# Casting x on VectorE with a loop staggered over four batches, loads and stores in order on one queue: a masked softmax of 16 matrix products

## The chip, the cores and the metric

The kernel runs on 1 core of a Trainium2 chip. The metric is the device time in microseconds (us), median of several runs; the profile covers one execution of them and its span is some 1.8 us shorter than the time measured for that execution (before: 92.4 of 94.16). Engines: PE = TensorE, DVE = VectorE, ACT = ScalarE, POOL = GpSimd, SP = the sync engine, which here only issues transfers. A profile page cuts the span into 40 equal slices: a digit of an engine's row is its busy time in tenths, PEclk is the clock that TensorE was granted in tenths of its full speed, DMA the busy share of the transfer engines, GB/s what they moved.

## The reference

```python
batch, m, k, n = 16, 512, 512, 512          # x float32, weight [k, n], scale 0.125
y = scale * np.matmul(x, weight)
y = np.where(mask == 1, y, -1e9)            # mask: strictly below the diagonal
y_exp = np.exp(y - np.max(y, axis=-1, keepdims=True))
return y_exp / np.sum(y_exp, axis=-1, keepdims=True)
```

A batch brings 1 MB of x in and takes 1 MB of result out. The exponentials are small enough here that the kernels leave the maximum out.

## The kernel before

For each batch: load x, cast to bf16 on the way by a GpSimd transfer; transpose its 16 blocks on TensorE (`prepare`); copy the transposed halves from PSUM to SBUF, one on VectorE, one on ScalarE; multiply block row by block row, only up to the diagonal, with one more matmul that adds a mask of -512 on the diagonal block; exponentiate on ScalarE, with row sums; scale by the reciprocal of the sums on VectorE; store.

```python
X_BUFS = 16
    def load(b):
        xb = x_pool.tile([P, MT, K], BF16, name="xb")
        nc.gpsimd.dma_start(xb, x_r[b])
    ...
    def prepare(b):                                  # 16 transposes, two copies
        for h in range(2):
            pt = psum_t.tile([P, 2, M], BF16, name="pt")
            ...
            if h == 0: nc.vector.tensor_copy(xt[:, 0:2], pt)
            else:      nc.scalar.copy(xt[:, 2:4], pt)
    ...
    def normalise(b):
        nc.vector.reciprocal(rinv, st_sum.pop(b))
        for mt in range(MT):
            NC = (mt + 1) * P
            nc.vector.tensor_scalar_mul(ot[:, mt, :NC], ot[:, mt, :NC], rinv[:, mt : mt + 1])
    ...
    for b in range(B):
        if b + 1 < B: prepare(b + 1)
        multiply(b); normalise(b); store(b)
```

The program is not run in the order of its source. Each engine's instructions are put into an order when the program is built, and each engine then runs its list from top to bottom.

The softmax here doesn't subtract the row's maximum and nothing guards it: scores larger than these inputs give would overflow.

Of the kernel before, what the change touches and what calls it, by code (L numbers as in the profile page):

```python
# [1 line left out]

# [5 lines left out]

FP32 = mybir.dt.float32
BF16 = mybir.dt.bfloat16  # L10
AF = mybir.ActivationFunctionType
ALU = mybir.AluOpType

MASK_NEG = -512.0
P = 128
X_BUFS = 16
OUT_BUFS = 6


@with_exitstack  # L20
def kernel(
    ctx: ExitStack,
    tc: tile.TileContext,
    x: bass.AP,
    weight: bass.AP,
    scale: float,
    mask: bass.AP,
    out: bass.AP,
):






    nc = tc.nc

    B, M, K = x.shape
    K2, N = weight.shape
    assert K == K2 and N == 512 and K == 512 and M == 512  # L40
    MT = M // P
    KT = K // P

    const = ctx.enter_context(tc.tile_pool(name="const", bufs=1))
    x_pool = ctx.enter_context(tc.tile_pool(name="xf", bufs=X_BUFS))
    xt_pool = ctx.enter_context(tc.tile_pool(name="xt", bufs=2))
    sum_pool = ctx.enter_context(tc.tile_pool(name="sums", bufs=4))
    psum_t = ctx.enter_context(tc.tile_pool(name="psum_t", bufs=4, space=bass.MemoryType.PSUM))
    psum_y = ctx.enter_context(tc.tile_pool(name="psum_y", bufs=4, space=bass.MemoryType.PSUM))

    x_r = x.rearrange("b (mt p) k -> b p mt k", p=P)
    out_r = out.rearrange("b (mt p) n -> b p mt n", p=P)

    ident_bf = const.tile([P, P], BF16, name="ident_bf")
    w_f32 = const.tile([P, KT, N], FP32, name="w_f32")
    w_bf = const.tile([P, KT, N], BF16, name="w_bf")
    diag_f32 = const.tile([P, MT, P], FP32, name="diag_f32")
    diag_bf = const.tile([P, MT, P], BF16, name="diag_bf")
    ots = [const.tile([P, MT, N], FP32, name=f"ot{i}") for i in range(OUT_BUFS)]

    st_x, st_xt, st_py, st_sum = {}, {}, {}, {}

    def load(b):
        xb = x_pool.tile([P, MT, K], BF16, name="xb")
        nc.gpsimd.dma_start(xb, x_r[b])  # L65
        st_x[b] = xb

    def prepare(b):

        xb = st_x.pop(b)  # L70
        xt = xt_pool.tile([P, KT, M], BF16, name="xt")
        for h in range(2):
            pt = psum_t.tile([P, 2, M], BF16, name="pt")
            for kk in range(2):
                kt = 2 * h + kk
                for mt in range(MT):
                    nc.tensor.transpose(  # L77
                        pt[:, kk, mt * P : (mt + 1) * P],
                        xb[:, mt, kt * P : (kt + 1) * P],
                        ident_bf,  # L80
                    )
            if h == 0:
                nc.vector.tensor_copy(xt[:, 0:2], pt)  # L83
            else:
                nc.scalar.copy(xt[:, 2:4], pt)  # L85
        st_xt[b] = xt

    def multiply(b):
        xt = st_xt.pop(b)
        ot = ots[b % OUT_BUFS]  # L90
        rsum = sum_pool.tile([P, MT], FP32, name="rsum")
        for mt in range(MT):
            NC = (mt + 1) * P
            py = psum_y.tile([P, N], FP32, name="py")
            for kt in range(KT):
                nc.tensor.matmul(  # L96
                    py[:, :NC],
                    lhsT=xt[:, kt, mt * P : NC],
                    rhs=w_bf[:, kt, :NC],
                    start=(kt == 0),  # L100
                    stop=(kt == KT - 1),
                )
            nc.tensor.matmul(  # L103
                py[:, mt * P : NC],
                lhsT=ident_bf,
                rhs=diag_bf[:, mt],
                start=False,
                stop=True,
                skip_group_check=True,
            )  # L110
            nc.scalar.activation(  # L111
                out=ot[:, mt, :NC],
                in_=py[:, :NC],
                func=AF.Exp,
                bias=0.0,
                scale=float(scale),
                accum_out=rsum[:, mt : mt + 1],
            )
        st_sum[b] = rsum

    def normalise(b):
        ot = ots[b % OUT_BUFS]
        rinv = sum_pool.tile([P, MT], FP32, name="rinv")
# [4 lines that stand above are left out]
        nc.gpsimd.memset(ot[0:1, 0, :P], 1.0 / N)  # L128

    def store(b):  # L130
        nc.sync.dma_start(out_r[b], ots[b % OUT_BUFS])  # L131

    make_identity(nc, ident_bf)


    load(0)
    nc.sync.dma_start(w_f32, weight.rearrange("(kt p) n -> p kt n", p=P))
    for mt in range(MT):
        nc.sync.dma_start(diag_f32[:, mt], mask[mt * P : (mt + 1) * P, mt * P : (mt + 1) * P])
    for b in range(1, X_BUFS):  # L140
        load(b)

    for ot in ots:
        for mt in range(MT - 1):
            nc.gpsimd.memset(ot[:, mt, (mt + 1) * P :], 0.0)  # L145
        nc.gpsimd.memset(ot[0:1, 0, P:], 1.0 / N)  # L146

    prepare(0)
    for kt in range(KT):
        if kt % 2 == 0:  # L150
            nc.vector.tensor_copy(w_bf[:, kt], w_f32[:, kt])  # L151
        else:
            nc.scalar.copy(w_bf[:, kt], w_f32[:, kt])  # L153
    nc.vector.tensor_scalar(  # L154
        out=diag_bf,
        in0=diag_f32,
        scalar1=-MASK_NEG,
        scalar2=MASK_NEG,
        op0=ALU.mult,
        op1=ALU.add,  # L160
    )

    for b in range(B):
        if b + 1 < B:
            prepare(b + 1)
        multiply(b)
        normalise(b)
        store(b)
        if b + X_BUFS < B:
            load(b + X_BUFS)  # L170


# [1 line left out]
_INS = ['x', 'weight', 'scale', 'mask']  # L174
_OUTS = [((16, 512, 512), 'float32')]

_NUMBERS = {'scale': 0.125}


# [26 lines left out]
```

## Time and profile before

| | before |
|---|---|
| time, median | 94.33 us |
| span | 92.4 us |
| busy PE / ACT / DVE | 57.5 / 47.0 / 37.2 us |
| bytes through HBM | 34.87 MB |
| a batch's compute, where nothing holds it (57 to 80 us) | 3.29 us |
| a batch's transfers at 408 GB/s | 5.14 us |

The row DMA of the page (tenths of busy time in 40 slices) is full all through, and the compute engines are not: the transfers are the bound. The lines are in the prediction below.

### The profile page before, as it was taken

The page shows a single profiled execution, that of the slowest core. Times are in us where ns is not written, and L with a number is a line of the kernel's source. Part 1 is how long each engine was busy: PE and PEld are TensorE (multiplying, and loading weights), DVE is VectorE, ACT ScalarE, POOL GpSimd, SP SyncE. Part 2 cuts the span into 40 slices and gives each one's busy share as a digit, 9 for nine tenths or more (in the row PEclk, how much of TensorE's full clock was granted, in tenths as well). Part 3 has the DMA queues.
Part 4 walks back from the last instruction along what each step waited for, and adds up shares of the span by engine and source line. Part 5 has one row for each costly group of instructions (what it writes and reads, how often), then busy time and mean ns, then how long its engine had stood idle before and what let it go on. Part 6 is the DMA issues. An engine that isn't in the chain of part 4 may idle for free.

```text
span 92.4 us, 1586 instructions
## 1 busy us (share of the span) xinstructions
PE 57.5 (62%) x568; PEld 43.1 (47%) x576; DVE 37.2 (40%) x99; ACT 47.0 (51%) x147; POOL 25.3 (27%) x62
## 2 busy tenths in 40 slices
PE   0000599999999999900019774699999999600000
PEld 0000568867876876900016352576786786200000
DVE  0030212458546799300004217276845853650000
ACT  5040044998789873400034091899878878700000
POOL 5993333222333999800001001011101110110000
PEclk9999999999999999996555699999999999995555
DMA  1899999999999999999999999999999999999990
GB/s 27 335 220 191 208 206 206 206 206 207 206 206 207 208 208 206 206 206 283 290 286 291 285 337 403 397 407 403 408 406 407 401 407 407 409 408 410 408 353 33
DMA packets 18007, 26.57 MB, mean 288 GB/s; under 512 B 592, under 2 KB 9296, under 8 KB 18000
## 3 DMA queue, kind: packets, MB, share of 16 engines
q0 software_dynamic: 8448, 8.39, 54.7%
q1 hardware_dynamic: 9552, 18.09, 52.5%
q8 instruction: 4, 0.07, 0.3%
q14 instruction: 3, 0.02, 0.1%
HBM read 18.09 MB, written 16.78 MB: 377 GB/s over the span
## 4 chain that ended last, share of the span: by engine, by line
DMA 44%; PE 23%; POOL 17%; DVE 1%; issue 1%; ACT 1%; DVEq 0%; SPq 0%; ACTq 0%; POOLq 0%
DMA xb<-in_x_dram 24%; DMA out_dram<-ot 20%; PE py L96 17%; POOL xb L65 7%; POOL ot L145 7%; PE pt L77 5%; POOL ot L146 2%; PE py L103 2%; DVE ot L127 1%; ACT ot L111 1%; POOL ot L128 1%; POOL ident_bf masks.py:199 0%; DVEq L201 0%; SPq L131 0%; POOL ident_bf masks.py:197 0%
## 5 line engine op out<-in xcount | busy, mean ns | idle before, releaser
L96 PE MATMUL py<-w_bf,xt 128*128 128x128 bf16 (+3 forms) x248 | 42.6, 310 | 12.2 <-ACT ot L111 11.6
L111 ACT ACTIVATE ot<-py 128x128 f32<-128x128 f32 (+1 forms) x64 | 27.5, 443 | 18.2 <-DMA out_dram<-ot 14.9
L96 PEld LDWEIGHTS <-xt 128*128 128x128 bf16 x256 | 22.2, 102 | 21.5 <-issue 13.4
L77 PE MATMUL pt<-ident_bf,xb 128*128 128x128 bf16 x256 | 18.1, 230 | 10.2 <-DMA xb<-in_x_dram 10.2
L127 DVE TENSOR_SCALAR ot<-ot,rinv 128x128 f32<-128x128 f32 (+1 forms) x64 | 23.2, 445 | 1.6 <-DVE rinv L124 0.5
L85 ACT COPY xt<-pt 128x1024 bf16<-128x1024 bf16 x16 | 16.2, 1016 | 10.8 <-PE pt L77 8.5
L77 PEld LDWEIGHTS <-xb 128*128 128x128 bf16 x256 | 16.3, 104 | 11.6 <-DMA xb<-in_x_dram 10.2
L83 DVE COPY xt<-pt 128x1024 bf16<-128x1024 bf16 x16 | 11.0, 689 | 15.9 <-PE pt L77 14.2
L65 POOL DMA_DIRECT2D xb<-in_x_dram x16 | 12.2, 770 | 16.4 <-DMA xb<-in_x_dram 16.1
L128 POOL MEMSET ot<- 1x128 f32 x16 | 4.3, 287 | 39.4 <-DVE ot L127 39.4
L103 PE MATMUL py<-diag_bf,ident_bf 128*128 128x128 bf16 x64 | 14.4, 225 | 0.0
L111 ACT ACTIVATION_READ_ACCUMULATOR ot<-py 128x1 f32 x64 | 13.4, 210 | 0.0
L124 DVE RECIPROCAL rinv<-rsum 128x4 f32<-128x4 f32 x16 | 2.7, 172 | 18.1 <-ACT ot L111 18.1
L103 PEld LDWEIGHTS <-ident_bf 128*128 128x128 bf16 x64 | 6.5, 102 | 3.4 <-issue 0.5
L145 POOL MEMSET ot<- 128x384 f32 (+2 forms) x18 | 6.3, 383 | 0.0
L151 DVE CAST w_bf<-w_f 128x512 bf16<-128x512 f32 x2 | 0.9, 481 | 5.9 <-DMA w_f<-in_weight_dram 5.9
L153 ACT CAST w_bf<-w_f 128x512 bf16<-128x512 f32 x2 | 1.1, 616 | 3.9 <-DMA w_f<-in_weight_dram 3.9
L146 POOL MEMSET ot<- 1x384 f32 x6 | 2.4, 408 | 0.0
L154 DVE TENSOR_SCALAR diag_bf<-diag_f 128x512 bf16<-128x512 f32 x1 | 0.4, 427 | 3.6 <-DMA diag_f<-in_mask_dram 3.6
L153 ACT ACT_TABLE_LOAD x1 | 1.3, 1283 | 0.7 <-PEq L187 0.7
masks.py:199 POOL TENSOR_SCALAR_AFFINE_SELECT ident_bf<-ident_bf 128x128 bf16<-128x128 bf16 x1 | 0.3, 307 | 0.1
masks.py:197 POOL MEMSET ident_bf<- 128x128 bf16 x1 | 0.2, 206 | 0.3 <-POOLq L187 0.3
(4 smaller groups left out, 0.4 us busy)
## 6 DMA issues: line engine op xcount, KB each, us to landing
out_dram<-ot SPq DMA_DIRECT2D x16, 1024.0 KB, 11.6
xb<-in_x_dram POOLq DMA_DIRECT2D x16, 512.0 KB, 21.0
w_f<-in_weight_dram SPq DMA_DIRECT2D x1, 1024.0 KB, 5.1
diag_f<-in_mask_dram SPq DMA_DIRECT2D x4, 64.0 KB, 6.5
```

The source lines that it names most:

```text
L65: nc.gpsimd.dma_start(xb, x_r[b])
L77: nc.tensor.transpose(pt[:, kk, mt * P : (mt + 1) * P], xb[:, mt, kt * P : (kt + 1) * P], ident_bf,)
L83: nc.vector.tensor_copy(xt[:, 0:2], pt)
L85: nc.scalar.copy(xt[:, 2:4], pt)
L96: nc.tensor.matmul(py[:, :NC], lhsT=xt[:, kt, mt * P : NC], rhs=w_bf[:, kt, :NC], start=(kt == 0), stop=(kt == KT - 1),)
L103: nc.tensor.matmul(py[:, mt * P : NC], lhsT=ident_bf, rhs=diag_bf[:, mt], start=False, stop=True, skip_group_check=True,)
L111: nc.scalar.activation(out=ot[:, mt, :NC], in_=py[:, :NC], func=AF.Exp, bias=0.0, scale=float(scale), accum_out=rsum[:, mt : mt + 1],)
L124: nc.vector.reciprocal(rinv, st_sum.pop(b))
L127: nc.vector.tensor_scalar_mul(ot[:, mt, :NC], ot[:, mt, :NC], rinv[:, mt : mt + 1])
L128: nc.gpsimd.memset(ot[0:1, 0, :P], 1.0 / N)
L145: nc.gpsimd.memset(ot[:, mt, (mt + 1) * P :], 0.0)
L146: nc.gpsimd.memset(ot[0:1, 0, P:], 1.0 / N)
```

## The change

The cast leaves the transfer and becomes a VectorE instruction; x is loaded as fp32 on the same queue that stores the results; the loop is staggered so that at step i the cast is for batch i+2, the transposes for i+1, the multiplication for i and the normalisation for i-1. The buffers for x go from 16 (bf16) to 5 (fp32).

```diff
-X_BUFS = 16
+X_BUFS = 5
     def load(b):
-        xb = x_pool.tile([P, MT, K], BF16, name="xb")
-        nc.gpsimd.dma_start(xb, x_r[b])
+        xf = x_pool.tile([P, MT, K], FP32, name="xf")
+        nc.sync.dma_start(xf, x_r[b])
+    def cast(b):
+        xb = xb_pool.tile([P, MT, K], BF16, name="xb")      # 3 buffers
+        nc.vector.tensor_copy(xb, st_x.pop(b))
 ...
-    for b in range(B):
-        if b + 1 < B:
-            prepare(b + 1)
-        multiply(b)
-        normalise(b)
-        store(b)
+    for i in range(B + 1):
+        if i + 2 < B:
+            cast(i + 2)
+        if i + 1 < B:
+            transpose(i + 1)
+        if i < B:
+            multiply(i)
+        if i >= 1:
+            normalise(i - 1)
+            store(i - 1)
+            if i - 1 + X_BUFS < B:
+                load(i - 1 + X_BUFS)
```

(Cut: set-up of the pool for the cast tiles, `cast(0)`, `transpose(0)` and `cast(1)` ahead of the loop, and the identity matrix made after the loads are issued.)

More of the change, by code (lines that the diff above doesn't have):

```diff
@@ L45 @@
     x_pool = ctx.enter_context(tc.tile_pool(name="xf", bufs=X_BUFS))
+    xb_pool = ctx.enter_context(tc.tile_pool(name="xb", bufs=3))
     xt_pool = ctx.enter_context(tc.tile_pool(name="xt", bufs=2))
@@ L59, with transpose @@
     ots = [const.tile([P, MT, N], FP32, name=f"ot{i}") for i in range(OUT_BUFS)]
-    st_x, st_xt, st_py, st_sum = {}, {}, {}, {}
+    st_x, st_xb, st_xt, st_sum = {}, {}, {}, {}
     def load(b):
-        xb = x_pool.tile([P, MT, K], BF16, name="xb")
-        nc.gpsimd.dma_start(xb, x_r[b])
-        st_x[b] = xb
-    def prepare(b):
-        xb = st_x.pop(b)
+        xf = x_pool.tile([P, MT, K], FP32, name="xf")
+        nc.sync.dma_start(xf, x_r[b])
+        st_x[b] = xf
+    def cast(b):
+        xb = xb_pool.tile([P, MT, K], BF16, name="xb")
+        nc.vector.tensor_copy(xb, st_x.pop(b))
+        st_xb[b] = xb
+    def transpose(b):
+        xb = st_xb.pop(b)
         xt = xt_pool.tile([P, KT, M], BF16, name="xt")
@@ L131, in store @@
         nc.sync.dma_start(out_r[b], ots[b % OUT_BUFS])
-    make_identity(nc, ident_bf)
     load(0)
@@ L141 @@
         load(b)
+    make_identity(nc, ident_bf)
     for ot in ots:
@@ L146 @@
         nc.gpsimd.memset(ot[0:1, 0, P:], 1.0 / N)
-    prepare(0)
+    cast(0)
+    transpose(0)
     for kt in range(KT):
@@ L161 @@
     )
-    for b in range(B):
-        if b + 1 < B:
-            prepare(b + 1)
-        multiply(b)
-        normalise(b)
-        store(b)
-        if b + X_BUFS < B:
-            load(b + X_BUFS)
+    cast(1)
+    for i in range(B + 1):
[10 more added lines that the diff above has]
+                load(i - 1 + X_BUFS)
 _INS = ['x', 'weight', 'scale', 'mask']
```

## The prediction

> **What bounds the kernel now.** I read the page first (slices, queues), then busy time by stretch, then the timeline, for the duration of each step.
>
> ```profile
> span 92.4 us, 1586 instructions
> ...
> PE   0000599999999999900019774699999999600000
> ...
> PEclk9999999999999999996555699999999999995555
> DMA  1899999999999999999999999999999999999990
> GB/s 27 335 220 191 208 206 206 206 206 207 206 206 207 208 208 206 206 206 283 290 286 291 285 337 403 397 407 403 408 406 407 401 407 407 409 408 410 408 353 33
> ...
> HBM read 18.09 MB, written 16.78 MB: 377 GB/s over the span
> ```
>
> One slice is 2.31 us. The DMA row is full from the second slice to the last but one; TensorE has two idle stretches that cost nothing. In slices 5 to 18 only loads run: 206 GB/s counted as bf16 landed, so 412 GB/s of fp32 read. From slice 25 only stores run, at some 407. Between, the mixture moves 290 counted. Everything is 18.09 + 16.78 = 34.87 MB, and 34.87 / 0.408 = 85.5 us: the transfers are the bound, with about 7 us of start, first slices and end around them. The compute engines need much less: PE 57.5, ACT 47.0, DVE 37.2 us busy, and in the stretch from 57 to 80 us a batch takes 3.29 us (transposes start at 64.24 and again at 67.53), with TensorE the limit. A batch's transfers need 2.097 MB / 0.408 = 5.14 us. So compute has 1.85 us to spare per batch, if its steps overlap.
>
> The lengths of those steps, from the timeline (start, length, engine, line, operation, count):
>
> ```profile
> 64.19 0.22 PE L103 MATMUL py<-diag_bf,ident_bf 128*128 128x128 bf16 x1
> ...
> 64.24 1.06 PE L77 MATMUL pt<-ident_bf,xb 128*128 128x128 bf16 x16
> ...
> 64.89 0.69 DVE L83 COPY xt<-pt 128x1024 bf16<-128x1024 bf16 x1 [0.86 <-PE pt L77]
> ...
> 67.47 0.22 PE L103 MATMUL py<-diag_bf,ident_bf 128*128 128x128 bf16 x1
> ...
> 67.73 0.60 ACT L111 ACTIVATE ot<-py 128x512 f32<-128x512 f32 x1 [0.23 <-PE py L103]
> ...
> 80.72 0.18 DVE L124 RECIPROCAL rinv<-rsum 128x4 f32<-128x4 f32 x1 [0.83 <-ACT ot L111]
> 80.99 1.29 DVE L127 TENSOR_SCALAR ot<-ot,rinv 128x128 f32<-128x128 f32 x4
> ```
>
> From the first transpose to the copy that empties the first half: 0.65 us (64.24 to 64.89). The batch's matmuls: 65.14 (first line of that group) to 67.47 + 0.22, so 2.55 us. Last exponential to reciprocal: 80.00 to 80.72, so 0.72. Reciprocal to first scaling: 0.27; four scalings: 1.29.
>
> **What the Trainium skill says.** "DMA: Bandwidth & Descriptors", section "SWDGE vs HWDGE vs iDMA": a cast during a DMA can only be issued from GpSimd; plain transfers may go by the sync queue. Section "Issuing engines are not separate DMA queues": all issuers share the same 16 engines. The trace agrees as far as it goes: software-queue loads read 412 GB/s, hardware-queue stores write 408. So I give the new queue no gain in rate. "VectorE: DVE Perf Modes", section "The perf-mode tier table": an fp32 SBUF copy of 2048 elements takes 1227 ns. The trace has no such size; its two casts of 512 took 0.88 us together, 0.44 each, and 1536 more elements at two per cycle of 0.96 GHz (the page's clock) add 0.80: 1.24. I take 1.23, an estimate. "TensorE: Matmul & The Clock Gate", Part 1: an idle array falls to half clock and needs a stretch of work to recover. The trace agrees: after TensorE stopped at 39.35 us the granted clock was 0.50 from 43 us, and it stayed so until 52, over 3 us into the next work.
>
> **The change part by part.**
> - Removed: the bf16 cast in the loads; 16 issues on GpSimd of 0.77 us. Neither bounds anything but the first 9 us, where slices 2 to 4 moved only about 2.1 MB of source data in 6.9 us. Worth about 1.7 us at the start (7 us at 408 GB/s would move 2.8 MB).
> - Moved: x as fp32 on the sync queue, 5 buffers instead of 16. Bytes through HBM are unchanged. After the first five, load n+5 is issued behind store n.
> - Added: 16 casts on VectorE, 16 x 1.23 = 19.7 us: 37.2 + 19.7 = 57 us of 92, no bound by itself.
> - The stagger: the source lets the cast run two batches ahead and the normalisation one behind. But the built program isn't in source order. I listed VectorE's instructions as built (batch numbers counted by me):
>
> ```
> Reciprocal(6)  cast(7)  scale(6) x3  copy xt(7)  scale(6)
> Reciprocal(7)  scale(7)  cast(8)  scale(7) x3  copy xt(8)
> Reciprocal(8)  cast(9)  scale(8) x3  copy xt(9)  scale(8)
> ```
>
> From batch 5 on, the cast of n+1 stands **behind the reciprocal of n**, except cast 11, ahead of reciprocal 10. TensorE's built order is transposes(n), all matmuls(n), transposes(n+1). An engine runs in order, so a closed ring arises: reciprocal(n) -> cast(n+1) -> transposes(n+1) -> copy to xt -> matmuls(n+1) -> last exponential -> reciprocal(n+1). Nothing of one batch overlaps the next in it, and prefetched loads can't shorten it.
>
> Length of the ring, when the cast follows at once: reciprocal to next operation 0.20; cast 1.23; three scalings 0.90 (longer than the 0.65 for the first transposes, so they hide it); copy 0.69; weight load 0.06 (11.99 to 12.05 in the start of the trace); matmuls 2.55; 0.03 to the exponential; 0.72. Sum 6.38 us. The other half of xt, on ScalarE, is ready about 0.94 + 0.2 + 1.02 = 2.2 us after the cast, while the matmuls that need only the first half run, and adds nothing. With one scaling ahead of the cast: 0.27 + 0.25 + 1.23 + 1.0 + 0.69 + 0.06 + 2.55 + 0.75 = 6.80. With the cast already done: 0.27 + 0.90 + 0.69 + 0.06 + 2.55 + 0.75 = 5.22. Reciprocal 5 to 15 is five of 6.80, four of 6.38 and one of 5.22: 64.7 us, against 51.4 that the transfers would need.
>
> The start: the first load is issued at about 0.75 and lands near 5.5 (the weights took 5.1 from issue to landing), the weights behind it near 8.1, their casts and the first copy end near 10, and the first matmuls run at half rate (the trace's first 16 transposes took 1.89 us instead of 1.06), so reciprocal 0 comes near 14.8. The casts are a batch or two ahead there; walking the built lists step by step with the same lengths puts reciprocal 5 near 36. End: 36 + 64.7 = 100.7; scaling 0.27 + 1.29; the last store of 1 MB alone some 4.7 (an estimate from the 5.1 of the weights); span 107. The measured time was 94.33 for a span of 92.4, so 1.9 more: **109 us**, 15% slower.
>
> **The rivals.**
> - *Transfers still bound it.* Five loads are in flight and 5.14 us a batch is generous; if the ring is under 5.1 us, the span is about 2.1 + 34.87 / 0.405 + 0.7 for a bubble ahead of the last stores + 2 = 91, time 92.8. Mixing loads and stores could cost some: between 47.75 and 53.17 the mixture moved 290 counted, about 190 of it store (one store's buffer came free at each of those times), so 390 of source, 4% under the pure rates; then 94 to 95. For it: DMA has always been the bound. Against: it needs 1.2 to 1.7 us off a sum of measured steps.
> - *VectorE's total is the bound*: per batch 1.23 + 0.69 + 0.27 + 1.29 = 3.5 us, below 5.14. No.
> - *The clock falls.* In the ring TensorE works 0.94 + 2.4 of 6.6 us with a pause of about 2.4 us. In the trace the clock fell 3 to 3.7 us after work stopped, so I expect it to hold. If it fell for good, matmuls and transposes add about 3 us per batch: 120 and more.
>
> **Range and chances.** The ring's sum has seven terms good to about 0.3 us together: ten rounds, 3 us; the start is good to 3 us; a lowered clock now and then adds up to 7. So 102 to 116. A prediction within 2% needs the ring to be wrong by 1.2 us a batch: 0.04; faster by 2% needs also a better transfer rate: 0.03.
>
> **What would show it.** Right: DMA row at 7 to 8 tenths in the middle, DVE waiting in total tens of us on ACT (at the reciprocal), TensorE waiting on DVE casts, periods of 6.3 to 6.8 us between reciprocals, cast at 1.2 us, no long wait of the casts for loads. Wrong: a full DMA row and casts that wait for loads (the first rival), or PEclk at 5 for most of the span (the third). The estimate fails most easily if the cast isn't 1.23 us, or if loads land so late that the ring isn't what ends last.

## The result

The changed kernel takes 114.94 us (113.28 to 116.26, 4 runs, the two longest of them counted as slow), before 94.33 (94.16 to 94.41). The ratio is 1.209, 95% interval 1.195 to 1.223. Ratios here are the mean time of one kernel's fast runs over that of the other's fast runs in the same rounds, so not quite the ratio of the medians. The time lies inside the predicted range of 102 to 116, at its upper end, 6 us above the predicted 109.

The page of the changed kernel, the rows that answer to those shown of before (here a slice is 2.83 us):

```profile
span 113.0 us, 1605 instructions
...
PE   0009959999765593846928379483956928379000
...
DVE  0076367796781904629055392608219045380500
...
PEclk9999999999999769996799958999596799958985
DMA  2998999999999999999999999989970900909072
GB/s 26 375 384 292 402 388 387 399 387 359 273 372 411 399 408 407 409 409 410 404 410 409 395 395 405 337 308 252 391 279 6 352 19 20 351 16 355 0 282 89
```

The GB/s row holds to the 25th slice; from the 31st on there are single transfers with nothing between. From the 15th slice on PE and DVE tend to take turns (9 over 0, 9 over 0 again, 2 over 5, 9 over 2): a first sign that they wait for each other. The waits (engine, line, what it waited for: total us, times, longest):

```profile
DVE rinv L131 <- ACT ot L118: 42.1, 14, 4.4
...
PE pt L84 <- DVE xb L73: 30.7, 12, 8.3
...
DVE xb L73 <- DMA xf<-in_x_dram: 8.3, 2, 6.1
```

VectorE waits 42 us at the reciprocal for the exponentials; TensorE waits 31 us for casts; the casts themselves waited for a load only twice, in the start. The data was there. One round of the ring, from the timeline:

```profile
57.76 0.18 DVE L131 RECIPROCAL rinv<-rsum 128x4 f32<-128x4 f32 x1 [4.14 <-ACT ot L118]
57.85 1.20 DVE L73 CAST xb<-xf 128x2048 bf16<-128x2048 f32 x1
...
59.10 1.07 PE L84 MATMUL pt<-ident_bf,xb 128*128 128x128 bf16 x16 [2.10 <-DVE xb L73]
...
59.78 0.67 DVE L90 COPY xt<-pt 128x1024 bf16<-128x1024 bf16 x1
...
60.51 1.16 PE L103 MATMUL py<-w_bf,xt 128*128 128x128 bf16 x9 [0.34 <-DVE xt L90]
...
63.12 0.60 ACT L118 ACTIVATE ot<-py 128x512 f32<-128x512 f32 x1
...
63.84 0.18 DVE L131 RECIPROCAL rinv<-rsum 128x4 f32<-128x4 f32 x1 [2.99 <-ACT ot L118]
```

Read the starts downwards: every line begins when the one above it has delivered what it needs or has freed its engine, and the last line is the first one again, one batch and 6.08 us later. The transfers of a batch would need 5.14.

Not every round is so short. Of the ten from reciprocal 5 (36.34 us) to reciprocal 15 (105.55 us), six take 7.5 to 7.7 us. The stretches of 1 us around one of them show why (columns: stretch, length, busy us and instructions of PE, weight loads, DVE, ACT and POOL, granted clock, DMA share, GB/s):

```profile
50.00:51.00 1.00, 0.00 (x0) 0.00 (x0) 0.81 (x3) 0.07 (x1) 0.28 (x1) 1.00 1.06 410
51.00:52.00 1.00, 0.15 (x2) 0.15 (x3) 1.00 (x3) 0.00 (x0) 0.93 (x1) 0.79 1.05 410
52.00:53.00 1.00, 1.00 (x12) 1.00 (x11) 0.88 (x4) 0.00 (x0) 0.00 (x0) 0.50 1.04 404
...
54.00:55.00 1.00, 0.93 (x6) 0.28 (x5) 0.00 (x0) 0.83 (x1) 0.00 (x0) 0.50 1.04 395
55.00:56.00 1.00, 1.00 (x11) 0.78 (x11) 0.00 (x0) 0.65 (x4) 0.00 (x0) 1.00 1.06 410
```

TensorE paused for about 2.5 us while VectorE scaled and cast, its clock fell to one half, and the transposes and the first matmuls ran at that rate for 3 us. In the five rounds with a scaling ahead of the cast the pause was 2.45 to 2.51 us, and the clock fell each time. But with the cast directly behind the reciprocal it was 2.10 to 2.11 us, and there the clock fell in one round of four, when the transposes already ran:

```profile
77.96 1.07 PE L84 MATMUL pt<-ident_bf,xb 128*128 128x128 bf16 x16 [2.10 <-DVE xb L73]
```

```profile
78.00:79.00 1.00, 1.00 (x16) 0.85 (x16) 1.00 (x4) 0.00 (x0) 0.34 (x1) 0.94 0.84 227
79.00:80.00 1.00, 0.66 (x6) 0.52 (x6) 0.70 (x2) 0.90 (x1) 0.00 (x0) 0.50 1.03 352
```

So the length of the pause doesn't decide alone. The falls come at 37.93, 51.58, 65.24, 78.89, 85.72 and 99.37 us: two or four times 3.41 us lie between one and the next, and each low stretch lasts 3.41 us. This points to a fixed grid of time, on which it matters where a pause lies; no run here moved a pause on purpose. The four runs line up with their mean clock: 0.908 for 113.28 us, 0.894 and 0.895 for 114.81 and 115.06, 0.881 for 116.26.

### The profile page after: what moved, and what is told of

The parts are those of the page before. It is cut to its first block, busy times and chain, and to the rows that moved or that the text cites. A ratio compares the mean times of both kernels' runs of the same rounds, so it can differ in the third digit from the quotient of the medians.

```text
span 113.0 us, 1605 instructions
## 1 busy us (share of the span) xinstructions
PE 68.6 (61%) x576; PEld 46.2 (41%) x576; DVE 53.7 (47%) x115; ACT 49.3 (44%) x147; POOL 18.3 (16%) x46
## 5 line engine op out<-in xcount | busy, mean ns | idle before, releaser
L103 PE MATMUL py<-w_bf,xt 128*128 128x512 bf16 (+3 forms) x256 | 47.2, 330 | 5.5 <-DVE xt L90 5.0
L84 PE MATMUL pt<-ident_bf,xb 128*128 128x128 bf16 x256 | 22.0, 254 | 30.7 <-DVE xb L73 30.7
L84 PEld LDWEIGHTS <-xb 128*128 128x128 bf16 x256 | 18.8, 116 | 35.0 <-DVE xb L73 34.8
L73 DVE CAST xb<-xf 128x2048 bf16<-128x2048 f32 x16 | 20.4, 1273 | 8.3 <-DMA xf<-in_x_dram 8.3
L135 POOL MEMSET ot<- 1x128 f32 x16 | 9.8, 614 | 87.7 <-DVE ot L134 75.0
L134 DVE TENSOR_SCALAR ot<-ot,rinv 128x128 f32<-128x128 f32 (+1 forms) x64 | 21.8, 385 | 0.8
L118 ACT ACTIVATION_READ_ACCUMULATOR ot<-py 128x1 f32 x64 | 12.8, 200 | 0.0
```

Of the source, the lines that this page charges most:

```text
L73: nc.vector.tensor_copy(xb, st_x.pop(b))
L84: nc.tensor.transpose(pt[:, kk, mt * P : (mt + 1) * P], xb[:, mt, kt * P : (kt + 1) * P], ident_bf,)
L103: nc.tensor.matmul(py[:, :NC], lhsT=xt[:, kt, mt * P : NC], rhs=w_bf[:, kt, :NC], start=(kt == 0), stop=(kt == KT - 1),)
L118: nc.scalar.activation(out=ot[:, mt, :NC], in_=py[:, :NC], func=AF.Exp, bias=0.0, scale=float(scale), accum_out=rsum[:, mt : mt + 1],)
L135: nc.gpsimd.memset(ot[0:1, 0, :P], 1.0 / N)
```

## The experiments

**Theory.** VectorE's built order (cast of n+1 behind the reciprocal of n) closes a ring through three engines (VectorE, TensorE, ScalarE), and the ring's length is the period. **Rival A:** five buffers and one queue in order starve the transfers. **Rival B:** VectorE has simply too much to do. All experiments give correct results. "Held" below means that each instruction is pinned behind the previous one of its engine in source order; that fixes the list:

```diff
+    keep = tc.keep_in_program_order
-        nc.vector.tensor_copy(xb, st_x.pop(b))
+        keep(nc.vector.tensor_copy(xb, st_x.pop(b)))
 (the same for every instruction on VectorE, TensorE, ScalarE and for the transfers on SP)
```

| run | order on VectorE | x buffers | median us | ratio to before |
|---|---|---|---|---|
| changed kernel | as built: cast behind the reciprocal | 5 | 114.94 | 1.209 |
| e1_source_order | held, source: cast two batches ahead of the multiplication, three ahead of the reciprocal | 5 | 112.59 | 1.191 |
| e5_source_order_6 | the same | 6 | 99.22 | 1.051 |
| e2_source_order_10 | the same | 10 | 96.19 | 1.019 |
| e8_source_10_cast_twice | the same, each cast twice | 10 | 95.89 | one run |
| e3_ring_10 | held: cast behind the reciprocal | 10 | 163.26 | 1.731 |
| e7_ring_10_warm | the same, extra matmuls in the pause | 10 | 128.09 | one run |
| e4_cast_early_5 | held: cast just ahead of the reciprocal | 5 | 103.77 | 1.100 |
| e6_ten_buffers_only | as built | 10 | 96.14 | 1.021 |
| e9_best_7, e10_best_8 | held, source, start mended | 7, 8 | 95.91, 95.85 | 1.017, 1.017 |

The kernel before took 94.3 to 94.4 us beside all of them.

### e1: the order of the source, five buffers

> The changed kernel with every VectorE, TensorE, ScalarE and sync-queue instruction held in the order of its source (cast two batches ahead of the normalisation, on every batch), still 5 x buffers. Theory (a closed ring through VectorE's built order sets the period): the ring is cut, reciprocals come every 5.1 to 6 us, time 95 to 103 us. Rival A (5 buffers and one queue in order starve the transfers): nothing changes, 113 to 116. Rival B (VectorE has too much work): the work is the same, so 113 to 116.

Measured 112.59 us: outside the theory's range and near the rivals'. The ring is gone, and another limit appears at nearly the same time. One line of its waits, then of its timeline:

```profile
DVE xb L74 <- DMA xf<-in_x_dram: 43.6, 15, 6.3
```

```profile
56.87 1.23 DVE L74 CAST xb<-xf 128x2048 bf16<-128x2048 f32 x1 [2.48 <-DMA xf<-in_x_dram]
...
62.37 1.23 DVE L74 CAST xb<-xf 128x2048 bf16<-128x2048 f32 x1 [2.20 <-DMA xf<-in_x_dram]
```

From 44.85 us on each cast waits over 2 us for its load. The cast of batch n+3 stands ahead of the scaling of n, hence of store n, hence of load n+5, which is behind the store on the queue and needs the buffer. So only two periods lie between the landing of load n+3 and that of load n+5. The nine reciprocals from 46.59 to 94.30 us come every 5.96 us on average. Casting further ahead uses the prefetch up: rival A is right for this order, though not for the built one.

### e5 and e2: six and ten buffers

```diff
-X_BUFS = 5
+X_BUFS = 6      # e5;  10 in e2
```

> As e1_source_order with one x buffer more (6). In e1 a second ring showed: load n+5 is issued behind store n, which stands behind the cast of n+3, so only two periods lie between the landing of load n+3 and of load n+5: 2 x 5.9 us measured. Theory: with 6 buffers there are three periods, 11.7 / 3 = 3.9 us, below the 5.14 us of the transfers, so these bind again: 95 to 97 us, like e2. Rival (5 buffers were not the reason, something in the single queue was): 105 or more.

> As e1_source_order, with 10 x buffers instead of 5. Theory: the transfers are the bound again, DMA row full, 91 to 95 us. If e1 stays above 97 and this one falls to 91 to 95, then behind the ring lay a second limit, the number of x buffers. Rival B (VectorE's total): 110 or more.

With one buffer more 99.22 us, with ten 96.19, 2.2 and 1.2 us above the expected ranges (95 to 97, 91 to 95). With six, reciprocals come every 5.1 us from the sixth on (45.05, 50.13, 55.20), so the steady state is that of the transfers, as expected; what it loses against e2 it loses around the fourth reciprocal (28.01, then 34.35), where slices 10 to 13 of its page move only 263 to 338 GB/s, and at the end, where slices 35 to 39 move 278 to 382. With ten, the page of e2 shows the transfers full to the end:

```profile
DMA  2897999999999999999999999999999999999940
GB/s 27 333 402 214 365 402 388 388 385 388 388 385 386 386 400 411 392 408 408 405 408 402 409 408 409 408 410 408 408 402 407 408 406 411 407 410 406 411 174 7
```

So the staggered loop works as intended only with order and buffers both: 96.19 us, and even then 1.9% above the kernel before.

### e3 and e7: the ring with ten buffers, without and with work in its pause

The source was rewritten so that it names VectorE's built order, the same for all batches, and was held (shortened: guards and keep left out):

```diff
 def normalise(b):
     nc.vector.reciprocal(rinv, st_sum.pop(b))
+    cast(b + 1)
     for mt in range(MT):
+        if mt == MT - 1: transpose(b + 1)
         nc.vector.tensor_scalar_mul(...)
-for i in range(B + 1): ...
+for b in range(B): multiply(b); normalise(b); store(b); load(b + X_BUFS)
-X_BUFS = 5
+X_BUFS = 10
```

> The order in which the changed kernel was built, made regular by hand for all batches (cast of n+1 behind the reciprocal of n, TensorE strictly transposes, matmuls, transposes), held so, with 10 x buffers. Theory: more prefetch can't shorten the ring; periods of 6.1 to 7.7 us for all 15 steps, 115 to 126 us. Rival A (buffers starve the transfers): 92 to 98.

Measured 163.26 us: prefetch doesn't help the ring at all, so rival A is out for the built order; but the theory had expected 115 to 126. Part of the difference is TensorE's list. The built program runs first the matmuls that need only VectorE's half of xt; held in source order, each batch also waits 0.4 to 0.8 us for ScalarE's half. The clock row of its page and two reciprocals:

```profile
PEclk9999955585585559576556858555765955555685
```

```profile
62.74 0.18 DVE L132 RECIPROCAL rinv<-rsum 128x4 f32<-128x4 f32 x1 [5.38 <-ACT ot L119]
72.20 0.18 DVE L132 RECIPROCAL rinv<-rsum 128x4 f32<-128x4 f32 x1 [6.14 <-ACT ot L119]
```

A round takes 8.9 to 9.8 us, most of it at half clock. To see whether the clock is the cause, e7 puts 24 matmuls into the pause; nobody reads their result, and they only add work:

```diff
+    dummy = psum_d.tile([P, P], FP32, name="dummy")        # psum_t: 3 buffers instead of 4
 def multiply(b):
     ...
+    for _ in range(24):
+        nc.tensor.matmul(dummy, lhsT=ident_bf, rhs=ident_bf, start=True, stop=True)
```

> e3_ring_10 with 24 extra matmuls (identity by identity, into a PSUM bank that nobody reads) behind each batch's matmuls, where TensorE waits for the cast. e3 took 163 us, periods of 9.0 to 9.5 us at a mean granted clock of 0.66. Theory (the ring's pauses let the clock fall, and that lengthens the ring): although work is added, the clock stays near 1, periods fall to 6.6 to 7.0 us, 125 to 132 us. Rival (the matmul order of e3 is slow at any clock): 163 us or more.

Measured 128.09 us, one run:

```profile
PEclk9999999999999999999999999999999999999975
```

```profile
64.63 0.18 DVE L137 RECIPROCAL rinv<-rsum 128x4 f32<-128x4 f32 x1 [3.69 <-ACT ot L122]
71.41 0.18 DVE L137 RECIPROCAL rinv<-rsum 128x4 f32<-128x4 f32 x1 [3.69 <-ACT ot L122]
```

All 15 rounds take 6.73 to 6.79 us, as expected. More work made the kernel 35 us faster. Both statements stand: the ring alone costs 6.8 us a round in this matmul order, and its pause costs 2 to 3 us more where it lets the clock fall. (e7 also has one PSUM buffer fewer for the transposes; what that does alone was not tried.)

### e4: only the cast moved, ahead of the reciprocal

```diff
 for b in range(B):
     multiply(b)
+    cast(b + 1)
     normalise(b)        # its own cast(b + 1) left out, else as e3
-X_BUFS = 10
+X_BUFS = 5
```

> As the built order of the changed kernel, with 5 buffers, one thing moved: the cast of n+1 stands directly ahead of the reciprocal of n instead of behind it. Theory: the cast leaves the ring, period 5.1 to 5.4 us, 99 to 105 us. Rival A or B: 113 to 116.

Measured 103.77 us with the same five buffers and the same queue as the changed kernel. The profiled run is a slow one (105.75), by one round of 7.05 us with a lowered clock; the rounds after it, for example:

```profile
75.89 0.18 DVE L132 RECIPROCAL rinv<-rsum 128x4 f32<-128x4 f32 x1 [1.86 <-ACT ot L119]
81.04 0.18 DVE L132 RECIPROCAL rinv<-rsum 128x4 f32<-128x4 f32 x1 [1.86 <-ACT ot L119]
```

5.15 us each. Against the changed kernel the buffers, the queue and the work are the same, and 11 us come back; against e3, which is held in the same way, the cast has moved by one place and there are fewer buffers, and 59 us come back. Neither rival explains that. The second pair is the cleaner one: the changed kernel's other engines run in a somewhat different order, and nothing is held there.

### e8: each cast twice

```diff
         nc.vector.tensor_copy(xb, xf)
+        nc.vector.tensor_copy(xb, xf)        # in e2_source_order_10
```

> e2_source_order_10 with every cast done twice: VectorE gets 1.23 us more per batch, 4.7 in all, still under the 5.14 us of the transfers. Theory (VectorE's total isn't the bound, the cast costs only where the order puts it on the path): 96 to 98 us. Rival B (each us of VectorE work counts): 96 + 16 x 1.23 = 116 us.

Measured 95.89 us in one run, no slower than e2:

```profile
PE 57.6 (61%) x576; PEld 42.0 (45%) x576; DVE 71.9 (76%) x131; ACT 47.6 (51%) x147; POOL 15.0 (16%) x46
```

VectorE is busy 71.9 us against 53.9 in e2, and the time doesn't move: rival B is out. In this order the cast costs nothing, since it is off the path.

### e6: ten buffers and nothing else

```diff
-X_BUFS = 5
+X_BUFS = 10
```

> The changed kernel with one number changed, 10 x buffers instead of 5, nothing held in order. Its built order then has the cast one to two batches ahead, as in the source. Theory (order decides): 94 to 98 us. A rival (buffers alone matter, the order doesn't) is already against e3_ring_10; this run shows what the one number does to both.

Measured 96.14 us. Nothing is held here, and yet VectorE's built order is another one, with the cast three batches ahead of the reciprocal, as in the source (the expectation says one to two):

```
cast(8)  Reciprocal(5)  scale(5) x4  copy xt(8)  cast(9)  Reciprocal(6)  scale(6) x4  copy xt(9)
```

The number of buffers set the order of the instructions. So the 19 us between the changed kernel and this one can't be read as the worth of prefetch: e3 has the same ten buffers.

### e9 and e10: an attempt to beat both

e2 with 7 or 8 buffers; the first batch multiplied ahead of the second's transposes; the four mask loads made one:

```diff
-    for mt in range(MT):
-        nc.sync.dma_start(diag_f32[:, mt], mask[mt * P : (mt + 1) * P, mt * P : (mt + 1) * P])
+    nc.sync.dma_start(diag_f32, bass.AP(mask.tensor, mask.offset, [[N, P], [P * N + P, MT], [1, P]]))
+    multiply(0)                              # ahead of the loop
```

> An attempt to beat both kernels: e2's held order with 7 x buffers, the four mask loads as one (so that no load waits for a completion slot at 7 us), and the first batch's matmuls ahead of the second's transposes. In e2 the third slice moved only 214 GB/s (about 1.1 us lost) and loads alone ran at 387 GB/s against 408 for loads and stores together (ten loads, about 1.1 us lost). Theory: both come back in part, 93.5 to 95 us, so level with the kernel before; under 92.4 would be a clear gain and is not expected.

> As e9_best_7 with 8 x buffers: tells whether 7 still starves the transfers a little (e5 with 6 did, 99 us against 96). If 7 is enough this is the same or 0.3 us slower, 93.5 to 95.5; if not, faster by up to 1 us.

95.91 and 95.85 us: both above what was expected of them, and 1.7% above the kernel before. The dip in the fourth slice (the expectation says third) stayed, at 219 and 199 GB/s, so its cause was not what the expectation calls waiting for a completion slot. (In e2 the sync queue waited 2.3 us for the weights to land before it issued a further load; in e9 and e10 it no longer does. No view shows a slot.) What the cause is remains open. Seven buffers are enough. No version found here beats the kernel before; its transfers are already full, and this change moves the same bytes.

## Why the prediction was right, point by point

- **What bounds the kernel.** Right before the change (transfers) and after it (the ring). The views that decided were the built order on VectorE and the durations in the timeline, not the busy shares, which look harmless in both kernels.
- **The cast: 1.23 us.** Its median in the changed kernel is 1.216 us. Only the first took 2.18 us; why is not shown.
- **The start: reciprocal 0 near 14.8, reciprocal 5 near 36.** Measured 15.44 and 36.34 us.
- **The ring.** For the cast directly behind the reciprocal 6.38 us were predicted; three of the four such rounds took 6.08 to 6.09, the fourth, with a lowered clock, 7.50. For the cast already done 5.22; measured 5.15. With one scaling ahead of the cast 6.80; all five took 7.62 to 7.71, none at full clock. The ten together: 64.7 predicted, 69.2 measured. At full clock the ring is thus 0.3 us shorter than its sum. Its VectorE steps were added at full length, but each starts some 0.1 us before the end of the one ahead of it (57.85, 58.96, 59.78 above).
- **The step that failed** is the third rival: "In the trace the clock fell 3 to 3.7 us after work stopped, so I expect it to hold." It didn't. The clock fell in six of ten rounds, five times in a pause of 2.45 to 2.51 us and once around one of 2.10 us. The five with a scaling ahead of the cast cost 38.3 us against 34.0; that is 4.3 of the 4.5 us by which the ring's term was too small. The cost of the clock itself is larger, some 7 us by my estimate: 1.4 for the round of 7.50 against 6.08, and some 1.15 for each of the five, if they too would be 0.3 under their sum at full clock. The range had up to 7 us for this. That the 109 us lie only 6 off is in part luck: the ring's steps taken too long hid some 3 us of it.
- **A sign that misled:** a DMA row of 7 to 8 tenths in the middle was to show the ring, a full one the first rival. The row stayed at 9, at 405 GB/s from 36 to 70 us, and yet no cast waited for a load there. By my count of the issues on SP against the GB/s, some 3.7 MB of transfers stood in the queue at 36 us and 1.5 MB at 70. The waits told the two apart, not the row.
- **The last store.** 4.7 us were taken; from the end of the last scaling (107.1) to the end of the span it was 5.9. With 0.3 in the start, 4.5 in the ring and 1.2 here, the span of 113.0 against 107 is accounted for.
- **The first rival (transfers still bound it)** did not come for the changed kernel, but it names what e2 showed: 94 to 95 for the mixture, 96.19 measured.
- **Not foreseen:** the order of the source, which the prediction took as the good one, has a ring of its own with five buffers (e1, 5.96 us a period). The prediction's argument that five loads in flight are generous counts only where the cast runs one batch ahead.

## What to carry to other kernels

Where a framework orders instructions, list what each engine really runs, and look for a cycle that leaves an engine at one place and returns to it one step later: its length is a period that no prefetch shortens, and the cure is one instruction moved. A stagger in the source is no stagger until the built order shows it, and each batch that a stage runs ahead takes one buffer from the prefetch. TensorE's pauses in such a cycle can cost twice, by the pause and by the clock that falls in it.

## What the Trainium skill lacked or had wrong

- "TensorE: Matmul & The Clock Gate", section "Why this matters for your kernels", warns of pauses over about 3 us between matmul bursts. Here shorter ones were enough: in the changed kernel a pause of 2.5 us (up to 51.85) brought the clock to 0.50 by the stretch from 52 us, and one of 2.10 us (up to 77.96) was followed by a fall at 78.89. In e3 waits of about 2.1 us for the cast, with a further 0.4 to 0.8 for ScalarE's copy, kept the mean clock at 0.66. With waits of 0.77, 0.34 and 0.52 us per round (e7) it stayed at 1.00.
- "DMA: Bandwidth & Descriptors" says that issuing from several engines saves only issue time; its rates are of transfers that it doesn't call casting, so a load that casts has none. Here loads alone ran mostly at 385 to 388 GB/s from the sync queue as fp32 (e2) and at 412 GB/s of source from GpSimd with the cast (before); loads and stores together on the sync queue ran at some 408. Why loads alone are slower on the sync queue is open.
- No page says that the number of buffers may change the order in which a built program issues its instructions: 5 against 10 was 114.94 against 96.14 us, with another order on VectorE.
